# Putting TensorE's instructions into the order of the program text, in a two-block transformer kernel

## The chip, the cores and the metric

The kernel runs on one core of a Trainium2 chip. Its time is the device time of one execution in microseconds; the runs before the change have a median of 1624.3 us. A core has a matrix engine (TensorE, PE in the rows), three engines for elementwise work (VectorE or DVE, ScalarE or ACT, GpSimd or POOL), and SyncE (SP), which here issues the transfers. Each engine works through a list of its own, in the order of that list, and waits at semaphores for the others. The kernel uses PSUM, into which TensorE writes, as eight banks of 128 x 512 fp32; ScalarE and VectorE read the banks out.

## The reference, cut to what matters

Two transformer blocks, one behind the other, on x of 512 tokens by 1024, in fp32:

```
# block 1
h = rms_norm(x, norm1); cols = split(h @ w_in)
y = concat[ short_conv(...), sparse_attention(q, compressed, selected, window keys, gates),
            latent_attention(c_q, c_kv, k_rope), stick_breaking(q, k, v) ]     # 256 columns each
x = x + group_rms_norm(y) @ w_out
x = x + square(relu(rms_norm(x) @ ffn_w1)) @ ffn_w2                            # 4096 hidden
# block 2
o  = gla(q, k_f, f_f, v) + reversed gla(...)        # 4 heads, chunks of 64
o  = rms_norm(o) * silu(g);  y_rec = o @ w_br_rec
qa, ka = partial_rotary(q_a), partial_rotary(k_a)   # 8 query heads, 2 key heads of 64
y_att = window_gqa_sink(qa, ka, va, sink) @ w_br_att
x = x + (sigmoid(gate_r) * y_rec + sigmoid(gate_a) * y_att) @ w_out
x = x + softmax(q @ k.T / 16) @ v @ w_o             # 4 heads over 256 memory tokens
x = x + conv_ffn(rms_norm(x))                       # 2816 hidden
```

In the stick-breaking heads, log(1 - sigmoid) of the logits is summed over the keys to the right of each key. In the sparse attention, blocks of 32 keys and values are compressed by a two-layer network before a first attention looks at them.

## The kernel before, in words

**Precision.** An fp32 product is made of three matmuls on rounded parts, hi x hi, lo x hi and hi x lo, which add up in one PSUM bank (`mm3`, L183 to L185). A part `hi` is a rounded copy by ScalarE (L191, L194, weights L258), a part `lo` the difference, by VectorE (L192, L195, weights L259). Weights come by SyncE's DMAs into three buffers `wraw` and are split there into two pairs `whi`, `wlo` (`wunit`).

**Layout.** A token-major result (tokens on partitions) is turned by TensorE's transposes, four of 128 x 128 into one bank, before it can be used in the next product. `trans_hl` (L854) then splits it with one ScalarE and one VectorE instruction. `trans_pair` (L866) makes operands for two heads from one bank; for each of the two parts ScalarE writes one half of the partitions and VectorE the other half (`split_pair`):

```
for i, s in enumerate("hl"):
    nc.scalar.activation(x[own], b[own], AF.Copy, scale=scale[own])            # L880
    nc.vector.scalar_tensor_tensor(x[oth], b[own], scale[own], x[own], ...)    # L881
```

**Banks.** Four banks with the tag `mm` take the projections. The other four are shared out by phase: two `L` for logits, one `pT` for transposes and one `o` for products with the values in both blocks' mixers. A tile with the same tag that is asked for again waits until the one before it in that bank has been read.

**Order.** The program text is a trace: Python functions issue instructions, and a scheduler then sets each engine's order, by a priority (the place in the trace) and by times that it models. The text interleaves by hand. Long projections are generators (`nproj_g`, `tproj_g`), which `fill`, `weave` and `pipeline` run some steps of between the steps of a head (`attend`: logits, softmax, transposes at L833, values at L844). In `mixers1`, the generator `side` runs beside the stick-breaking heads (first product L913 and L914, sums over keys L934, values L946): it projects queries and values, then two operands of the compression, which go from the bank through VectorE (L636, L637), two DMAs that shift partitions, VectorE (L1175), ScalarE and VectorE into `cB`, and then the compression's matmuls (L1184, L1186) and the projection of keys and values in turns. At its end `nsa_norms` normalises queries and keys (ScalarE, VectorE; the queries at L1015), and `nsa_prep` turns them with `trans_pair`. The generator `side2` runs beside the sparse attention with the convolution and the latent attention's projections. At the end of `mixers1`, `group_out` normalises the last group of columns (`yN`; squares at L785, scaled at L789) and turns it (L798) into H4 and H5, operands of the output projection; that of the group before becomes H6 and H7.

In `mixers2` the linear attention's heads (`gla_head`) are followed by `window`: VectorE rotates part of queries and keys (L1649 to L1652), four `trans_pair` turn the queries (`wq0` to `wq3`), two `trans_hl` the doubled keys (`wkd` to `wk0`, `wk1`), and then logits (L889, L890) and the rest of a head alternate with projections, of `rT` (the recurrent branch), merged with a gate in `M`. Its output `oN` is turned by four `trans_hl` ahead of the product with `w_br_att`.

## Time and profile before

| | us |
|---|---|
| median of 3 runs | 1624.3 (1623.17 to 1624.51) |
| profiled execution | 1626.29 |
| its span | 1624.6 |
| TensorE busy | 1591.5 (98%), 8049 matmuls and transposes |
| VectorE, ScalarE, GpSimd busy | 921.0 (57%), 667.0 (41%), 174.9 (11%) |
| mean DMA rate | 91 GB/s |

The stages by time of the span: first projection and stick-breaking to about 115 us, sparse and latent attention to about 282, first output projection and feed-forward layer to 690, linear attention to 912, window attention and output projection to about 1056, memory attention, and from about 1230 on the second feed-forward layer.

In the timelines below, a row gives start, length, engine, line, operation, output and inputs; in square brackets stands how long the engine had been idle before it and what ended that. Lengths of TensorE's rows overlap, since matmuls are pipelined: the step from one start to the next is what a matmul costs (0.23 us for 512 columns).

### The profile page before, as it was taken

Reading aid. Unit: us, or ns where it says so; the run is one execution under the profiler, and the core shown is the slowest. Engines: PE = TensorE matmul, PEld = TensorE weight load, DVE = VectorE, ACT = ScalarE, POOL = GpSimd, SP = SyncE. Lnnn points to the kernel's source line nnn. Section 1 sums busy time; section 2 is a strip of 40 time slices with the busy share of each in tenths; the row PEclk is TensorE's granted clock in tenths of the full one; section 3 lists DMA queues with packets and bytes.
Section 4 is the critical chain, followed back from the end, with each engine's and each line's share of the span. In section 5 each row is a group of like instructions: output and inputs, shape, how many; then the busy total and the mean of one; then the engine's idle time right before and its main releaser. Section 6 shows DMA issues by size and latency. Waiting matters only on the chain.

```text
span 1624.6 us, 20813 instructions
## 1 busy us (share of the span) xinstructions
PE 1591.5 (98%) x8049; PEld 1341.8 (83%) x8049; DVE 921.0 (57%) x1503; ACT 667.0 (41%) x1172; POOL 174.9 (11%) x185
## 2 busy tenths in 40 slices
PE   8999999999999999999999999999999999999998
PEld 6798888788888888878888788888988888888886
DVE  6666885644223434475766565664667556526662
ACT  5675554544123423334333354353544233222332
POOL 0121110200000001121110000330002111001110
PEclk9999999999999999999999999999999999999999
DMA  7242131232322223221222211323332333232331
GB/s 225 67 126 85 33 117 40 66 102 92 101 94 98 97 94 100 88 89 55 73 72 78 65 40 59 115 96 118 126 98 84 99 98 97 94 101 91 101 120 52
DMA packets 108118, 148.15 MB, mean 91 GB/s; under 512 B 7887, under 2 KB 58868, under 8 KB 108020
## 3 DMA queue, kind: packets, MB, share of 16 engines
q1 hardware_dynamic: 107876, 146.72, 28.3%
q8 instruction: 63, 1.03, 0.3%
q14 instruction: 35, 0.29, 0.1%
q10 hardware_dynamic: 144, 0.11, 0.0%
HBM read 142.31 MB, written 4.20 MB: 90 GB/s over the span
## 4 chain that ended last, share of the span: by engine, by line
PE 90%; DVE 4%; ACT 2%; issue 1%; POOL 1%; DMA 1%; SPq 0%; POOLq 0%; DVEq 0%; ACTq 0%
PE mm L183 25%; PE mm L185 25%; PE mm L184 25%; PE o L844 2%; PE lv L1570 2%; PE pT L833 1%; PE o L1613 1%; DVE wlo L259 1%; ACT whi L258 1%; PE L L889 1%; DMA wraw<-w_in_dram 1%; DMA wraw<-w_down_dram 1%; PE o L183 0%; PE o L185 0%; PE L L890 0%
## 5 line engine op out<-in xcount | busy, mean ns | idle before, releaser
L259 DVE TENSOR_TENSOR wlo<-wraw,whi 128x1024 fp32r<-128x1024 f32 (+4 forms) x268 | 319.5, 1194 | 439.2 <-ACT whi L258 434.5
L258 ACT ACTIVATE whi<-wraw 128x1024 fp32r<-128x1024 f32 (+4 forms) x268 | 270.4, 1010 | 536.9 <-PE mm L184 470.2
L417 POOL TENSOR_TENSOR nacc<-nacc,nsq 128x512 f32<-128x512 f32 x24 | 37.3, 1553 | 508.7 <-ACT nsq L415 507.6
L1866 POOL TENSOR_TENSOR fz<-fz,fu 128x512 f32<-128x512 f32 x22 | 37.4, 1698 | 269.6 <-ACT fz L1865 269.6
L461 DVE TENSOR_TENSOR x<-mm,x 128x512 f32<-128x512 f32 x72 | 48.9, 687 | 19.1 <-PE mm L185 18.8
L183 PE MATMUL mm<-H4h,whi 128*128 128x512 f32 x147 | 59.3, 404 | 0.0
L183 PE MATMUL mm<-H0h,whi 128*128 128x512 f32 x139 | 55.8, 402 | 2.9 <-ACT whi L258 2.9
L183 PE MATMUL mm<-H6h,whi 128*128 128x512 f32 x147 | 58.1, 399 | 0.4 <-ACT H6h L194 0.4
L183 PE MATMUL mm<-H7h,whi 128*128 128x512 f32 x147 | 58.3, 397 | 0.0
L185 PE MATMUL mm<-H4h,wlo 128*128 128x512 f32 x147 | 57.6, 392 | 0.7 <-DVE wlo L259 0.7
L183 PE MATMUL mm<-H5h,whi 128*128 128x512 f32 x147 | 58.1, 395 | 0.0
L185 PE MATMUL mm<-H6h,wlo 128*128 128x512 f32 x147 | 57.7, 393 | 0.0
L185 PE MATMUL mm<-H5h,wlo 128*128 128x512 f32 x147 | 57.7, 393 | 0.0
L184 PE MATMUL mm<-H6l,whi 128*128 128x512 f32 x147 | 57.7, 393 | 0.0
L184 PE MATMUL mm<-H5l,whi 128*128 128x512 f32 x147 | 57.4, 391 | 0.0
L184 PE MATMUL mm<-H4l,whi 128*128 128x512 f32 x147 | 57.4, 391 | 0.0
L185 PE MATMUL mm<-H7h,wlo 128*128 128x512 f32 x147 | 57.4, 390 | 0.0
L184 PE MATMUL mm<-H7l,whi 128*128 128x512 f32 x147 | 57.3, 390 | 0.0
L185 PE MATMUL mm<-H2h,wlo 128*128 128x512 f32 x139 | 54.5, 392 | 1.1 <-DVE wlo L259 1.1
L183 PE MATMUL mm<-H3h,whi 128*128 128x512 f32 x139 | 55.4, 399 | 0.0
L183 PE MATMUL mm<-H2h,whi 128*128 128x512 f32 x139 | 55.2, 397 | 0.0
L183 PE MATMUL mm<-H1h,whi 128*128 128x512 f32 x139 | 54.9, 395 | 0.0
(1264 smaller groups left out, 4340.1 us busy)
## 6 DMA issues: line engine op xcount, KB each, us to landing
wraw<-ffn_w_dram SPq DMA_DIRECT2D x64, 512.0 KB, 3.6
wraw<-w_up_dram SPq DMA_DIRECT2D x88, 256.0 KB, 2.8
wraw<-w_in_dram SPq DMA_DIRECT2D x36, 512.0 KB, 3.4
wraw<-w_down_dram SPq DMA_DIRECT2D x22, 512.0 KB, 3.6
wraw<-w_mem_kv_dram SPq DMA_DIRECT2D x16, 512.0 KB, 3.7
wraw<-w_in_dram SPq DMA_DIRECT2D x52, 128.0 KB, 2.3
wraw<-w_in_dram SPq DMA_DIRECT2D x20, 256.0 KB, 2.8
wraw<-cmp_w_dram SPq DMA_DIRECT2D x8, 512.0 KB, 4.0
```

What stands on the lines that cost most here:

```text
L183: mm(out, a.hi, b.hi, start=start, stop=False, skip_group_check=skip)
L184: mm(out, a.hi, b.lo, start=False, stop=False, skip_group_check=skip)
L185: mm(out, a.lo, b.hi, start=False, stop=stop, skip_group_check=skip)
L258: nc.scalar.activation(hi, raw, AF.Copy)
L259: nc.vector.tensor_sub(lo, raw, hi.bitcast(F32))
L417: eng.tensor_add(nm.acc, nm.acc, sq[:, :nm.N])
L461: self.nc.vector.tensor_add(self.x[k], b, self.x[k])
L833: nc.tensor.transpose(b[:, t * P:(t + 1) * P], st["p"][:, t * P:(t + 1) * P], self.ident)
L844: nc.tensor.matmul(o(), st["pT"][:, t * P:(t + 1) * P], v(t), start=(t == 0), stop=(t == nt - 1))
L889: self.nc.tensor.matmul(out, q[h][:, qs], k.hi[:, ks], start=True, stop=False)
L1570: nc.tensor.matmul(b[:, t * P:(t + 1) * P], ym[:, t * P:(t + 1) * P], mix(X, c, t * P, P), start=True, stop=True)
L1866: nc.gpsimd.tensor_mul(z, z, us[c])
```

## The change

The body of the first mixers behind the first projection, and the four stages that follow, are put into a context of the framework in which the scheduler keeps TensorE's instructions in the order in which the text issues them. The other engines' orders are still found by the scheduler, against the new order of TensorE. Everything else in the diff is indentation; lines behind L536 move by four or five.

```diff
-        self.ffn1()
+        with tc.manual_schedule(engines={mybir.EngineType.PE}):
+            self.ffn1()
...
-        self.mixers2()
+        with tc.manual_schedule(engines={mybir.EngineType.PE}):
+            self.mixers2()
...
-        self.memory()
+        with tc.manual_schedule(engines={mybir.EngineType.PE}):
+            self.memory()
...
-        self.ffn2()
+        with tc.manual_schedule(engines={mybir.EngineType.PE}):
+            self.ffn2()
...
             self.tproj(nm.H, w, [(1772, 512)], ev_sqk)
             self.setup_rest()
-            qN = self.T(mp, [P, NT, 256], F32, "qN")
-            svN = self.T(mp, [P, NT, 256], F32, "svN")
...
+            with tc.manual_schedule(engines={mybir.EngineType.PE}):
+                qN = self.T(mp, [P, NT, 256], F32, "qN")
+                svN = self.T(mp, [P, NT, 256], F32, "svN")
...
```

TensorE's list differs in two stretches, which are the mixers' second part (from about 74 us to the output projection at about 292) and the window attention with what follows (from 912 to about 1010), and in two short places of the memory attention. Three of the places follow, as TensorE's list has them.

TensorE at the start of the window attention, before the change, in part: the transposes of the queries `qkv` into `pT` stand one by one between projection matmuls of `rT0` and `rT1`.

```order
L183 MATMUL mm_7858<-rT0h_6626,whi_7862 128x512
L184 MATMUL mm_7858<-rT0l_6627,whi_7862 128x512
L185 MATMUL mm_7858<-rT0h_6626,wlo_7863 128x512
L183 MATMUL mm_7858<-rT1h_7061,whi_7862 128x512
L866 MATMUL pT_7774<-cmat_78,qkv_5936 128x128
L184 MATMUL mm_7858<-rT1l_7062,whi_7862 128x512
L185 MATMUL mm_7858<-rT1h_7061,wlo_7863 128x512
L866 MATMUL pT_7774<-cmat_78,qkv_5936 128x128
```

The same place after it, from the last transposes of the linear attention (`tr`) to the first projection matmul of `rT0`:

```order
L1639 MATMUL tr_7723<-cmat_78,go_7684 128x128 x4
L871 MATMUL pT_7782<-cmat_78,qkv_5944 128x128 x4
L871 MATMUL pT_7793<-cmat_78,qkv_5944 128x128 x4
L871 MATMUL pT_7804<-cmat_78,qkv_5944 128x128 x4
L871 MATMUL pT_7815<-cmat_78,qkv_5944 128x128 x4
L859 MATMUL pT_7829<-cmat_78,wkd_7826 128x128 x4
L859 MATMUL pT_7841<-cmat_78,wkd_7838 128x128 x4
L894 MATMUL L_7851<-wk0h_7834,wq0h_7787 128x256
L895 MATMUL L_7851<-wk0l_7835,wq0h_7787 128x256
L894 MATMUL L_7859<-wk0h_7834,wq0l_7790 128x256
L895 MATMUL L_7859<-wk0l_7835,wq0l_7790 128x256
L183 MATMUL mm_7865<-rT0h_6634,whi_7870 128x512
```

All 24 transposes of queries and keys moved ahead of the projection matmuls that had stood before and between them.

TensorE at the first step of the compression, before: behind the matmul that ends the projection of the compression's operands stand the sums over keys (L934) of a stick-breaking head.

```order
L185 MATMUL mm_649<-H7h_197,wlo_730 128x512
L934 MATMUL L_674<-sbLh_691,cmatr_81 128x512
L934 MATMUL L_674<-sbLl_692,cmatr_81 128x512
L934 MATMUL L_674<-sbLh_702,cmatr_81 128x384
L934 MATMUL L_675<-sbLh_702,cmatr_81 128x384
```

The same place after:

```order
L185 MATMUL mm_651<-H7h_197,wlo_732 128x512
L1189 MATMUL mm_765<-whi_743,cB_770 64x256
L1191 MATMUL mm_765<-wlo_744,cB_770 32x256
L1189 MATMUL mm_765<-whi_743,cB_770 64x256
L1191 MATMUL mm_765<-wlo_744,cB_770 32x256
L1189 MATMUL mm_765<-whi_743,cB_770 64x256
L1191 MATMUL mm_765<-wlo_744,cB_770 32x256
L1189 MATMUL mm_765<-whi_743,cB_770 64x256
L1191 MATMUL mm_765<-wlo_744,cB_770 32x256
L939 MATMUL L_676<-sbLh_693,cmatr_81 128x512
```

The first eight matmuls of the compression, which read `cB`, moved ahead of the sums over keys and of the next head's logits.

TensorE at the preparation of the sparse attention, before: the transposes of the normalised queries `qN` among projection matmuls that are already at the weights' second unit (`whi_1326`).

```order
L183 MATMUL mm_1322<-whi_1326,H3h_157 128x364
L184 MATMUL mm_1322<-wlo_1327,H3h_157 128x364
L866 MATMUL pT_1334<-cmat_78,qN_427 128x128
L185 MATMUL mm_1322<-whi_1326,H3l_158 128x364
L866 MATMUL pT_1334<-cmat_78,qN_427 128x128
L184 MATMUL mm_1323<-wlo_1327,H2h_147 128x364
```

The same place after:

```order
L1034 MATMUL pT_1275<-sbe_1270,rel_1272 4x384
L1205 MATMUL L_1281<-cmat_78,ev_1222 128x32 x4
L183 MATMUL mm_1323<-whi_1177,H0h_127 128x364
L184 MATMUL mm_1323<-wlo_1178,H0h_127 128x364
L185 MATMUL mm_1323<-whi_1177,H0l_128 128x364
L871 MATMUL pT_1336<-cmat_78,qN_429 128x128 x4
L183 MATMUL mm_1323<-whi_1177,H1h_137 128x364
L184 MATMUL mm_1323<-wlo_1178,H1h_137 128x364
L185 MATMUL mm_1323<-whi_1177,H1l_138 128x364
L871 MATMUL pT_1350<-cmat_78,qN_429 128x128 x4
```

The transposes moved ahead of nearly the whole first unit and part of the second; three matmuls stand ahead of them and three between the two batches.

## Rows read from the trace of the kernel before

**Rows 1.** The page's first part: busy time, share of the span, instructions.
```profile
PE 1591.5 (98%) x8049; PEld 1341.8 (83%) x8049; DVE 921.0 (57%) x1503; ACT 667.0 (41%) x1172; POOL 174.9 (11%) x185
```

**Rows 2.** The page's chain that ended last, by engine.
```profile
PE 90%; DVE 4%; ACT 2%; issue 1%; POOL 1%; DMA 1%; SPq 0%; POOLq 0%; DVEq 0%; ACTq 0%
```

**Rows 3.** Stretches: length, busy time of each engine, clock, DMA share, GB/s.
```profile
40.60:324.90 284.30, 272.55 (x1618) 233.63 (x1617) 193.70 (x466) 171.34 (x396) 52.02 (x85) 0.98 0.25 76
...
893.50:1015.00 121.50, 120.53 (x709) 102.38 (x708) 71.78 (x166) 58.40 (x130) 4.32 (x8) 1.00 0.17 54
```

**Rows 4.** Short stretches of TensorE alone: length, busy, clock, DMA share, GB/s.
```profile
178.00:181.40 3.40, 3.40 (x10) 0.51 0.03 7
283.60:287.10 3.50, 3.50 (x9) 0.52 0.00 0
...
74.05:81.68 7.63, 5.95 (x38) 1.00 0.50 138
```

**Rows 5.** Timeline of TensorE at the start of the window attention.
```profile
912.66 0.59 PE L1634 MATMUL tr<-cmat,go 128*128 128x128 f32 x2 [0.53 <-DVE go L1632]
913.01 0.48 PE L183 MATMUL mm<-rT0h,whi 128*128 128x512 f32 x1
...
929.53 0.63 PE L866 MATMUL pT<-cmat,qkv 128*128 128x128 f32 x4
...
933.31 0.63 PE L866 MATMUL pT<-cmat,qkv 128*128 128x128 f32 x4
```

**Rows 6.** Timelines of VectorE and ScalarE there.
```profile
918.49 0.32 DVE L1652 TENSOR_TENSOR qkv<-qkv,wu 128x160 f32<-128x160 f32 x1
...
930.20 0.69 ACT L880 ACTIVATE wq2h<-pT,w 64x512 fp32r<-64x512 f32 x1 [2.14 <-PE pT L866]
...
930.92 0.74 DVE L881 SCALAR_TENSOR_TENSOR wq2h<-pT,w,wq2h 64x512 fp32r<-64x512 f32 x1 [1.53 <-ACT wq2h L880]
...
931.69 0.68 ACT L880 ACTIVATE wq2l<-pT,w 64x512 fp32r<-64x512 f32 x1 [0.81 <-DVE wq2h L881]
...
932.41 0.76 DVE L881 SCALAR_TENSOR_TENSOR wq2l<-pT,w,wq2l 64x512 fp32r<-64x512 f32 x1 [0.75 <-ACT wq2l L880]
```

**Rows 7.** Timeline of TensorE ahead of the product with `w_br_att`.
```profile
1001.49 0.60 PE L854 MATMUL pT<-cmat,oN 128*128 128x128 f32 x4
...
1003.31 0.40 PE L183 MATMUL mm<-H1h,whi 128*128 128x512 f32 x1
1003.54 0.62 PE L854 MATMUL pT<-cmat,oN 128*128 128x128 f32 x4
```

**Rows 8.** Timeline of TensorE in the stick-breaking heads and the compression.
```profile
69.06 2.34 PE L946 MATMUL o<-svN,sba 128*128 128x64 f32 x20
...
74.05 0.39 PE L934 MATMUL L<-sbLh,cmatr 128*128 128x512 f32 x1
...
77.06 0.38 PE L934 MATMUL L<-sbLl,cmatr 128*128 128x256 f32 x1 [0.49 <-DVE sbLl L192]
...
81.68 0.31 PE L1184 MATMUL mm<-whi,cB 128*64 128x256 f32 x1
```

**Rows 9.** Timelines of TensorE and VectorE at the sparse attention's preparation.
```profile
116.53 0.28 PE L185 MATMUL mm<-whi,H7l 128*128 128x256 f32 x1
...
123.54 0.27 PE L866 MATMUL pT<-cmat,qN 128*128 128x128 f32 x1
...
122.71 1.49 DVE L1015 TENSOR_TENSOR qN<-qN,nrr 128x256 f32<-128x256 f32 x4
```

**Rows 10.** Timelines of TensorE and VectorE at the first mixers' end.
```profile
282.85 0.33 PE L798 MATMUL pT<-cmat,yq 128*128 128x128 f32 x1 [0.37 <-ACT yT L805]
283.60 1.97 PE L183 MATMUL mm<-H6h,whi 128*128 128x512 f32 x4 [0.42 <-ACT H6h L194]
...
291.60 0.48 PE L183 MATMUL mm<-H4h,whi 128*128 128x512 f32 x1
...
287.53 1.15 DVE L789 TENSOR_SCALAR yN<-yN,grs 128x256 f32<-128x256 f32 x4 [1.13 <-POOL grs L226]
```

## The prediction

> **What bounds the kernel now.** I read the page's first part, then its chain, then the table of stretches, and last the timeline at the places where TensorE's work moves. The first part says that TensorE is the bound: busy for 1591.5 of 1624.6 us, with VectorE at 57% and ScalarE at 41% [rows 1], and 90% of the chain that ended last is TensorE [rows 2]. So there is little to win and much to lose: whatever TensorE has to wait for comes straight on top of the time. The stretches tell how little. Between 40.6 and 324.9 us TensorE is idle for 284.30 - 272.55 = 11.8 us, and between 893.5 and 1015 us for 121.50 - 120.53 = 1.0 us [rows 3]. These two stretches are, apart from two short pieces in the memory attention, the only ones where the change gives TensorE another order; in the feed-forward layers and in nearly all of the linear attention the instructions stand as before.

> [...]

> **The change, place by place.** No instruction is added or taken away that counts; TensorE alone is put into the order in which the program was written down. Everything between the other engines stays nearly as it was, so I take durations from the rows and ask at each place what TensorE now has to do while it waits. What it did there before isn't lost: it comes later, so the loss is the work that no longer covers the wait.

> *Start of the window attention, +20 us (13 to 23).* Now six batches of four transposes stand one behind another, with not one projection matmul between them. They all write the one bank `pT`, so each waits until the batch ahead of it has been read out. The rows show one such round without a foreign engine's delay: transposes at 929.53, ScalarE 930.20, VectorE 930.92, ScalarE 931.69 (0.81 us of it waiting for VectorE), VectorE 932.41, next transposes at 933.31 [rows 5, 6]. That is 3.78 us a round. The first batch can't end before the last rotary step of VectorE at 918.49 + 0.32 = 918.81 [rows 6]; VectorE's own order up to there doesn't change. So: batch one at 918.9, ScalarE behind it at 919.2, then 3.11 us of reading out (930.20 to 933.31), so batch two at 922.3, three at 926.1, four at 929.9, the first batch of keys at 933.7. A batch of keys is read out in 1001.49 to 1003.54 = 2.05 us [rows 7], so the second stands at 935.7, the first logits at about 936.2, four of them, and the first projection matmul at about 936.6. Before, it ran at 913.01 [rows 5]. Of these 23.6 us, 24 transposes (0.11 us each) and four logits are work that was done later before, 3.1 us. That leaves 20.5, less half a microsecond of waiting that was there already (0.53 at 912.66). The low end has the rotary steps end 4 us earlier (as far as VectorE's other work could leave their way) and three rounds at 3.1 us, the bare reading out; the high end adds a slow clock during the transposes.

> *Stick-breaking heads and compression, +10 us (4 to 14).* At 74.05 us TensorE went on with the sums over keys of the first head (L934) [rows 8]. Now eight compression matmuls stand ahead of them, and these ran at 81.68, when their operand had passed VectorE, a DMA, VectorE, ScalarE and VectorE again [rows 8]. None of that chain gets shorter. TensorE waits through 7.63 us of which it was busy 5.95 before [rows 4]; by issue intervals (0.23 us for 512 columns, as 1003.31 to 1003.54 [rows 7]) that work is 4.4 us, so +4.4. For the next heads the chain from the end of the logits (69.06) to the last operand of L934 (77.06) is 8.0 us [rows 8]. The cover now standing in it is the value product (2.3 us [rows 8]), sixteen compression matmuls and six of 256 columns (2.6 us) in one head, and in the other the value product and eighteen matmuls (2.1), plus 0.8 us of L934 that needs only the first two operands. That leaves 2.3 and 2.8 us. Weight units of eight short matmuls may add another microsecond, since splitting one takes longer than using it. 4.4 + 2.3 + 2.8 + 0.5 = 10. The low end is the first wait alone; the high end has the heads at their bare 8 us less the value product.

> *Preparation of the sparse attention, +9 us (5 to 12).* The last value matmul of the projection starts at 116.53; the first transposes of the normalised queries stand at 123.54, as soon as VectorE has the first of four tiles (from 122.71) [rows 9]. In between, TensorE did projection matmuls that have 364 columns. Now only some 1.5 us of work stand ahead of the transposes: 7.0 - 1.5, less what VectorE and ScalarE may be earlier, is 4 to 5 us. The second batch waits for a round of 3.78 us with 0.4 us of transposes and 0.5 of matmuls in it: 2.8. The next two wait 1.5 and 0.7 by the same count. Low: the first wait alone; high: every round bare.

> *End of the first mixers, +5 us (3 to 7).* Eight transposes of the last group's output now stand ahead of 24 matmuls (H6, H7) that ran while the group was being normalised. TensorE gets there at 282.85; VectorE scales the four tiles at 287.53 to 288.68 [rows 10]. So it waits to 288.7, then a round of 2.05 us less 0.4 before the second four, and the 24 matmuls (5.4 us) end at about 296.7 where the next ones began at 291.6: 5.1.

> *Transposes in front of the attention's output projection, +5 us (3 to 6).* Four batches back to back where seven matmuls stood between two: 3 x (2.05 - 0.44) = 4.8 [rows 7].

> *Latent-attention projections and memory attention, +4 us (0 to 8).* Five transposes or products one behind another around 172 to 178 us and two places where an output bank is asked for again at once; at most a round of 2.05 us each, mostly covered by what stands between. I take 2 and 2.

> *The clock, +4 us (0 to 9).* The new waits will drop the clock two or three times more than before, at 1.7 us each; none at the low end, five times at the high one.

> *What is won back, -5 us (-12 to 0).* Waits and slow stretches of the old order in the places that change: 11.8 + 1.0 us of idle time and two stretches at 1.7 are 16.2 at most. Most of it sits at chains that stay as long as they are (the 0.49 us at 77.06 [rows 8]), so I take a third.

> **Sum.** 20 + 10 + 9 + 5 + 5 + 4 + 4 - 5 = 52. The profiled execution took 1626.29 us, so 1678.3; it is 2.0 above the median of the runs (1624.3), so 1676 for a median.

> **The rivals.**
> *The other engines catch up (1645 us).* VectorE, ScalarE and SyncE are ordered by the scheduler, and it knows TensorE's order: it can put the work that TensorE waits for ahead of weight splits. For it: VectorE is idle 43% of the time, so there is room. Against it: its order in the window's first 20 us is the old one, and the rounds are chains through one bank that no order shortens. The low ends with something won back, 13 + 4 + 5 + 3 + 3 + 0 + 0 - 7 = 21, give 1645.
> *The stalls feed on each other (1702 us).* High ends, with little won back: 23 + 14 + 12 + 7 + 6 + 8 + 9 - 1 = 78, so 1702. For it: two stretches at half clock stand in the old order already [rows 4], the second right behind waits of 0.37 and 0.42 us [rows 10]. Against it: in 74.05 to 81.68 TensorE was idle for 1.7 us and its clock stayed at 1.00 [rows 4]. [...]
> *Faster (1612 us).* The written order was interleaved by hand: projections are handed out between the steps of the heads, so it could keep TensorE busier than the scheduler's modelled times do. Its price is at most the 16.2 us above; three quarters of it is 12. It decides only if the six batches of the window find their data ready, and they can't before 918.81. So it needs the window's term under some 6 us and all others near nothing.
> *The change does nothing (1624 us).* It would have to leave TensorE's order alone; it does in 60% of the span, but not at the places above.

> **How the numbers follow.** Forecast case (1655 to 1695): 0.65. Others catch up: 0.16. Stalls feed on each other: 0.13. Faster: 0.03. Nothing: 0.03. 1676 is the first. The range goes from 1644 to 1698 and leaves out the faster cases, the lower part of the second and the upper of the third, about 0.19. A change of 0.2% (3 us) is about what can be told from none; slower by more has 0.94, within it 0.03, faster by more 0.03.

> **What would show it right or wrong.** In the new profile: TensorE idle for 18 us or more in the 25 us behind the last linear-attention transposes, its rounds 3 to 4 us apart and ended by ScalarE or VectorE; a wait of some 7 us at 74 us for `cB`; one of 4 us before the query transposes near 118 us and one of 5 to 6 near 283 us (both later by what was lost before); the feed-forward stretches free of idle time as before; PEclk below 1.0 behind the waits. I am wrong if the window's transposes have projection matmuls between them in time, if the wait before the compression is under 3 us, or if idle time in the unchanged stretches differs.

## The result: 1719.2 us, 5.8% slower

The changed kernel takes 1719.16 us (median of 4 runs, 1718.26 to 1719.29) against 1624.4 us for the kernel before on the same chip: a ratio of 1.0584, 95% interval [1.0566, 1.0602]. That is 43 us above the forecast of 1676 and 21 us above the end of its range. The sign was right, the size was not.

The first part of the page of the changed kernel gives busy time, share of the span and count for each engine, and its fourth part the chain that ended last; they answer to [rows 1] and [rows 2].

```profile
PE 1617.3 (94%) x8049; PEld 1360.2 (79%) x8049; DVE 926.0 (54%) x1503; ACT 669.4 (39%) x1172; POOL 168.0 (10%) x185
...
PE 82%; DVE 8%; issue 4%; ACT 3%; DMA 2%; POOL 1%; SPq 1%; POOLq 0%; DVEq 0%; ACTq 0%
```

These two numbers already split the loss. The span grew from 1624.6 to 1717.5 us, by 92.9. For the same 8049 instructions TensorE was busy 1617.3 - 1591.5 = 25.8 us longer: 23.5 of that goes with a lower granted clock, as the next table shows. Its idle time grew from 33.1 to 100.2 us, by 67.1: those are the waits. My sum had 4 and 48 for the two.

Next, the table of stretches. The first two rows are the two stretches of [rows 3] as they stand now (from and to the same instructions); columns are length, busy time of PE, PEld, DVE, ACT and POOL, granted clock, DMA share and GB/s.

```profile
40.80:373.50 332.70, 284.59 (x1614) 241.98 (x1615) 195.74 (x463) 170.38 (x394) 47.16 (x85) 0.93 0.21 65
943.60:1094.50 150.90, 127.64 (x708) 108.09 (x708) 72.15 (x166) 59.90 (x130) 3.57 (x8) 0.90 0.14 43
```

Idle time of TensorE went from 11.8 to 48.1 us in the first, and from 1.0 to 23.3 us in the second. The following rows are the same view of the stretches of the changed kernel in which the granted clock stood at its lower level: 0.50 in slices of one microsecond, 0.50 to 0.57 as the means of the stretches, which hold the edges. The last two or three microseconds of the span, where TensorE has no work left, are low in both kernels (0.50) and are set apart; four stretches of 3.4 us, full of work, are left out, the sum is over all eleven.

```profile
77.80:84.60 6.80, 4.28 (x18) 3.96 (x19) 3.44 (x7) 1.38 (x3) 0.00 (x0) 0.53 0.47 149
...
135.50:145.70 10.20, 5.85 (x23) 4.36 (x24) 6.25 (x15) 4.44 (x10) 4.39 (x13) 0.50 0.34 92
207.40:217.60 10.20, 9.84 (x34) 7.97 (x35) 5.27 (x18) 2.23 (x8) 0.00 (x0) 0.51 0.06 21
...
326.60:336.80 10.20, 5.70 (x17) 4.48 (x18) 3.23 (x8) 2.42 (x7) 1.02 (x1) 0.50 0.01 2
...
964.60:991.90 27.30, 10.09 (x34) 6.88 (x35) 12.55 (x30) 9.29 (x15) 1.50 (x5) 0.51 0.07 20
...
1169.50:1176.30 6.80, 4.67 (x11) 3.74 (x12) 2.67 (x4) 0.39 (x1) 1.04 (x1) 0.51 0.00 0
1282.80:1289.60 6.80, 6.63 (x28) 6.36 (x29) 1.66 (x4) 1.14 (x4) 0.00 (x0) 0.53 0.22 75
sum 91.90, PE 60.66 PEld 49.58 DVE 43.27 ACT 25.48 POOL 8.97; mean PE 5.51 PEld 4.51 DVE 3.93 ACT 2.32 POOL 0.82
```

There are eleven such stretches of 91.9 us with 60.7 us of TensorE's work in them. Taking half of that work as the price, they cost about 30 us: products of 512 columns start 0.43 us apart at the lower level (1175.18 to 1175.61 us) and 0.23 apart at 1.00 (1165.40 to 1165.63). The kernel before had four of 3.4 us at 0.50 to 0.52, full of work (two are in [rows 4]), which cost 6.8. The difference, 23.5, is close to the 25.8 of the page.

Last, the list of what TensorE waited for (total, times, longest).

```profile
PE mm L1189 <- DVE cB L192: 7.2, 1, 7.2
PE pt L439 <- DVE nsq L437: 5.2, 1, 5.2
PE pT L871 <- DVE qN L1020: 5.1, 1, 5.1
PE pT L803 <- DVE yN L794: 4.9, 1, 4.9
...
PE pT L859 <- DVE wq3l L886: 3.3, 1, 3.3
PE pT L871 <- DVE wq0l L886: 3.2, 1, 3.2
...
PE o L183 <- DVE H3l L192: 2.8, 1, 2.8
PE pT L838 <- ACT sbe L842: 2.5, 4, 1.5
PE mm L183 <- ACT mla_p L194: 2.2, 1, 2.2
```

The first, third and fourth are the waits that I had put at `cB`, at the query transposes and at the last group, close to the lengths I gave them (7, 4 to 5, 5 to 6 us). The second, in the memory attention, I had not seen.

To see where the delay is picked up, I took the start of each TensorE instruction after minus before; the clock's part of a place is half of the busy time in its slow stretches, less the same before.

| place | delay gained | clock in it | the rest | forecast for the rest |
|---|---|---|---|---|
| stick-breaking and compression | 15.0 | 3.8 | 11.2 | 10 |
| preparation of the sparse attention | 13.0 | 2.9 | 10.1 | 9 |
| sparse and latent attention | 14.6 | 3.3 | 11.3 | 2 |
| end of the first mixers | 7.1 | 1.2 | 5.9 | 5 |
| start of the window attention | 23.0 | 5.0 | 18.0 | 20 |
| transposes ahead of the output projection | 6.4 | 1.7 | 4.7 | 5 |
| memory attention | 13.1 | 5.7 | 7.4 | 2 |
| everything else | 0.7 | 0 | 0.7 | -5 (won back) |

The last row is made of 1.2 us by which this execution runs ahead at 20 us, 1.5 us lost in the linear attention and some 0.4 us lost behind the memory attention.

### The profile page after: what moved, and what is told of

It is laid out like the page before. It is cut to its first block, busy times and chain, and to the rows that moved or that the text cites. A ratio compares the mean times of both kernels' runs of the same rounds, so it can differ in the third digit from the quotient of the medians.

```text
span 1717.5 us, 20826 instructions
## 1 busy us (share of the span) xinstructions
PE 1617.3 (94%) x8049; PEld 1360.2 (79%) x8049; DVE 926.0 (54%) x1503; ACT 669.4 (39%) x1172; POOL 168.0 (10%) x185
## 4 chain that ended last, share of the span: by engine, by line
PE 82%; DVE 8%; issue 4%; ACT 3%; DMA 2%; POOL 1%; SPq 1%; POOLq 0%; DVEq 0%; ACTq 0%
PE mm L183 23%; PE mm L185 23%; PE mm L184 23%; PE o L849 2%; DVE wlo L259 1%; PE lv L1575 1%; PE pT L838 1%; ACT whi L258 1%; PE o L1618 1%; PE L L939 1%; PE L L894 1%; DMA wraw<-w_down_dram 1%; PE L L895 0%; PE o L183 0%; PE o L185 0%
## 5 line engine op out<-in xcount | busy, mean ns | idle before, releaser
L258 ACT ACTIVATE whi<-wraw 128x1024 fp32r<-128x1024 f32 (+4 forms) x268 | 270.3, 1010 | 551.8 <-PE mm L184 480.5
L1871 POOL TENSOR_TENSOR fz<-fz,fu 128x512 f32<-128x512 f32 x22 | 37.3, 1695 | 269.5 <-ACT fz L1870 269.5
L461 DVE TENSOR_TENSOR x<-mm,x 128x512 f32<-128x512 f32 x72 | 49.1, 688 | 23.5 <-PE mm L185 23.0
```

What stands on the lines that cost most here:

```text
L258: nc.scalar.activation(hi, raw, AF.Copy)
L461: self.nc.vector.tensor_add(self.x[k], b, self.x[k])
L1871: nc.gpsimd.tensor_mul(z, z, us[c])
```

## The experiments

### One part of the change at a time

In four kernels only one stage keeps TensorE's written order; all others lose it by edits like this one:

```
-        with tc.manual_schedule(engines={mybir.EngineType.PE}):
-            self.mixers2()
+        self.mixers2()
```

First mixers: 

> TensorE in the order of the text only in the first mixers behind the first projection; all other stages as before. If each place costs what the two traces show there (49.8 us of delay between 74 and 300 us of the old span, less 1.2 won at the start), the time is 1624 + 48 = 1672. If the losses of one stage depend on the others (for instance because the later stages recover some of it), it is under 1660 or over 1685.

Second mixers: 

> The order of the text only in linear attention and window attention. Places that stand for themselves: 1.5 + 23.0 + 6.4 = 31 us, so 1655. If the window's cost hung on delays brought along from the first mixers: 1640 or less.

Memory attention: 

> The order of the text only in the memory attention with the projection in front of it. Places that stand for themselves: 6.8 + 5.8 + 0.6 = 13 us, so 1637. My prediction's term for this stage was 2 us, so 1626; if the 13 us came from buffers or transfers displaced by earlier stages, it is there.

Both feed-forward layers: 

> The order of the text only in the two feed-forward stages. Both theories: no change, 1624 (within 2); a cost of the context itself, by semaphores or otherwise, would show here as over 1627.

Measured, against 1625.44 us for the kernel before: 1675.33 (ratio 1.0303 [1.0273, 1.0333]), 1656.19 (1.0186 [1.0156, 1.0215]), 1635.19 (1.0063 [1.0040, 1.0086]) and 1626.57 (1.0007 [0.9996, 1.0018]). The four differences, 49.9, 30.8, 9.8 and 1.1, make 91.6, and the whole change costs 94.8: the parts add up to within some 3 us, each with its own clock loss (mean granted clock 0.984, 0.986, 0.994 and 0.996). The two mixers and the feed-forward layers came as expected (1672, 1655, 1624). The memory attention costs 3 us less than the 13 expected, but far more than the forecast's 2.

### The first mixers in quarters

The kernel before, with the written order in one quarter of the first mixers, by these lines ahead of it and behind it. This was done when the 14.6 us of the sparse and latent attention still had no cause.

```
+            cm = tc.manual_schedule(engines={mybir.EngineType.PE})
+            cm.__enter__()
...
+            cm.__exit__(None, None, None)
```

Stick-breaking heads: 

> The kernel before, with TensorE in written order only in the stick-breaking heads and what runs beside them (40 to 114 us), the scheduler's order elsewhere. If each stretch pays for its own order: 12 us slower, 1637. If the work behind it takes up part of the delay: under 8 us.

Preparation of the sparse attention: 

> Written order only from the end of the heads through the preparation of the sparse attention (114 to about 150 us). If each stretch pays for its own order: 15 us slower, 1640. If the measured 15 us were in part handed down from the heads: under 10.

Sparse and latent attention: 

> Written order only in the sparse and the latent attention (about 150 to 275 us). If the 14 us of this stretch are waits of its own order: 1636 to 1640. If they are handed down from the stretches ahead, whose filler steps it lacks: under 5 us slower, 1625 to 1630.

End: 

> Written order only at the end of the first mixers (from the last group's normalisation). If each stretch pays for its own order: 8 us slower, 1633. The forecast's term for this place was 5.

Measured, against 1624.96: 1641.96 (1.0107 [1.0078, 1.0136]), 1634.73 (1.0066 [1.0043, 1.0089]), 1637.32 (1.0079 [1.0049, 1.0108]) and 1630.77 (1.0037 [1.0021, 1.0053]). So 17.0, 9.8, 12.4 and 5.8 us, together 45.0 of the 49.9, where 12, 15, 12 to 16 and 8 were expected. In the first, 2.1 of the 17.0 us are there by 48 us, most of them from a stretch at the lower clock (0.50 from 44 to 47 us), where the changed kernel's execution stands at 1.00. The second, 9.8, is by its time a case for losses handed down from the heads (under 10). Its trace says otherwise: TensorE waits 5.03 and 2.24 us for the two batches of query transposes, against 5.13 and 2.23 in the changed kernel; only the 1.8 us of waits for `kvN` ahead of them are missing. The third quarter costs 12 us by itself, so its waits are not handed down. Its rows say the same. TensorE's timeline in the changed kernel (start, length, line, and in brackets how long it had been idle and for whom):

```profile
196.07 0.70 PE L1119 MATMUL pT<-vbd,npc 128*128 128x256 f32 x2 [0.52 <-DVE sbe L844]
...
201.33 0.66 PE L803 MATMUL pT<-cmat,yN 128*128 128x128 f32 x4 [0.52 <-ACT sbe L842]
...
207.12 0.79 PE L183 MATMUL mm<-whi,mla_p 128*128 128x512 f32 x1 [2.24 <-ACT mla_p L194]
...
231.70 0.70 PE L1119 MATMUL pT<-vbd,npc 128*128 128x256 f32 x2 [1.34 <-DVE sbe L844]
...
254.57 0.66 PE L838 MATMUL pT<-cmat,sba 128*128 128x128 f32 x4 [1.49 <-ACT sbe L842]
```

And in the kernel with the written order in the third quarter alone:

```profile
169.78 0.70 PE L1117 MATMUL pT<-vbd,npc 128*128 128x256 f32 x2 [0.52 <-DVE sbe L842]
...
175.04 0.66 PE L801 MATMUL pT<-cmat,yN 128*128 128x128 f32 x4 [0.52 <-ACT sbe L840]
...
180.83 0.50 PE L183 MATMUL mm<-whi,mla_p 128*128 128x512 f32 x1 [2.24 <-ACT mla_p L194]
...
202.85 0.70 PE L1117 MATMUL pT<-vbd,npc 128*128 128x256 f32 x2 [1.34 <-DVE sbe L842]
...
225.72 0.66 PE L836 MATMUL pT<-cmat,sba 128*128 128x128 f32 x4 [1.49 <-ACT sbe L840]
```

The same waits, to a hundredth of a microsecond, 26.3 us earlier, and 28.9 us earlier from 202.85 on. The step between the two is the clock: behind the same wait for `mla_p` it stays low for 10.2 us in the changed kernel (0.51, the row from 207.40) and for 3.4 us here (0.50 from 183 to 185 us). The waits belong to that stretch's order: fifteen places where a transpose or a product stands right behind what feeds it. The same stretch in the kernel before and in this one (length and busy times; the stretch ends at the same instruction):

```profile
165.00:245.00 80.00, 75.94 (x464) 65.28 (x462) 63.65 (x181) 47.42 (x116) 13.72 (x16) 0.96 0.24 76
```

```profile
165.00:257.30 92.30, 78.90 (x477) 66.89 (x476) 67.76 (x185) 48.25 (x117) 13.13 (x16) 0.96 0.21 66
```

TensorE idles 13.4 us in place of 4.1 at the same mean clock of 0.96.

### The window's rounds

Both kernels are otherwise as the changed one. In the first, the projections are queued ahead of the window attention, and `WF` says how many of their steps are written behind each batch of transposes:

```
+WF = (8, 5, 5, 5, 5, 3, 3)
...
+            self.fill(WF[c])
```

> The changed kernel, with 34 steps of the projections written between the transposes of the window attention (8 ahead of the first batch, 5 between batches of queries, 5 and 3 at the keys, 3 behind) in place of none. Theory one, uncovered waits: what stood between the transposes in the old order is back, so the window's 23 us fall to 2 or less, 1698. Theory two, the chain of rotary steps and reading out is the bound wherever the projections stand: 1715 or more.

In the second, the four batches of queries go to different banks:

```
-            qT += self.trans_pair(wp, [qkv[:, t, c * P:(c + 1) * P] for t in range(NT)], eighth, f"wq{c}")
+            qT += self.trans_pair(wp, [qkv[:, t, c * P:(c + 1) * P] for t in range(NT)], eighth, f"wq{c}",
+                                  ps=("pT", "L", "o", "L")[c])
```

> The changed kernel, with the four batches of query transposes written to the banks pT, L, o, L in place of pT alone; nothing else. If the single bank sets the round: transposes no longer wait, ScalarE and VectorE work on different banks at once, 1.5 us a batch in place of 4.2, so some 8 us less with the clock, 1711. If ScalarE and VectorE are the bound with their 2.9 us a batch whatever the banks: 1716 to 1719.

Measured: 1700.09 us (1.0457 [1.0426, 1.0487]) and 1706.46 us (1.0496 [1.0465, 1.0526]), so 19.1 and 12.7 us less than the changed kernel's 1719.16. The first came as its first case had it, the second lies below both of its cases. Timeline of TensorE in the changed kernel:

```profile
968.91 0.47 PE L871 MATMUL pT<-cmat,qkv 128*128 128x128 f32 x1 [1.14 <-DVE qkv L1657]
972.62 1.09 PE L871 MATMUL pT<-cmat,qkv 128*128 128x128 f32 x4 [3.23 <-DVE wq0l L886]
976.85 1.09 PE L871 MATMUL pT<-cmat,qkv 128*128 128x128 f32 x4 [3.15 <-DVE wq1l L886]
981.09 1.09 PE L871 MATMUL pT<-cmat,qkv 128*128 128x128 f32 x4 [3.15 <-DVE wq2l L886]
985.43 1.09 PE L859 MATMUL pT<-cmat,wkd 128*128 128x128 f32 x4 [3.25 <-DVE wq3l L886]
988.02 1.09 PE L859 MATMUL pT<-cmat,wkd 128*128 128x128 f32 x4 [1.50 <-DVE wk0l L192]
```

Each round waits some 3.2 us for VectorE's last instruction on the bank, as the forecast said; but a batch lasts 1.09 us and not 0.63 [rows 5], and a round 4.23 and not 3.78. The kernel with steps between them, in its row of stretches:

```profile
965.00:992.00 27.00, 24.69 (x119) 19.72 (x119) 19.96 (x37) 10.96 (x16) 1.75 (x6) 1.00 0.28 79
```

TensorE works through 24.7 of 27 us, at a granted clock of 1.00. So rounds through one bank with nothing beside them are the cause of this place: cover gave back 19.1 us, more banks 12.7, two thirds of that. By the starts of TensorE's instructions 16.8 and 11.6 us of the two gains come in the window and the transposes behind it. Another 2.7 us in each come at the changed kernel's row from 1282.80, where neither kernel was edited. TensorE waits 2.76 us for `H3l` there in all three executions, but in these two the clock stays up. The kernel with steps between, with that wait inside, at 1.00:

```profile
1262.00:1272.00 10.00, 7.24 (x53) 6.66 (x52) 5.30 (x10) 4.07 (x10) 0.00 (x0) 1.00 0.32 105
```

So the same wait of 2.76 us has a slow stretch behind it in one execution and none in the other two, and 2.7 us of difference between the kernels come from that alone.

### The clock by itself

114 products of 512 columns that nobody reads are written into the bank `o` where TensorE waits (sparse preparation, end of the first mixers, window, memory broadcast). They add work and shorten no chain.

```
+        b = self.ps("o") if n else None
+        for _ in range(n):
+            self.nc.tensor.matmul(b, x[:, 0:P], x, start=True, stop=True)
```

> The changed kernel, with 114 matmuls of 512 columns added whose result nobody reads: in the waits of the sparse attention's preparation (16, 6, 3), of the first mixers' end (12, 5), of the window attention (8, 10, 10, 10, 10, 4) and ahead of the memory's token broadcast (18). They are 26 us of work put into 45 us of waits; no wait is shortened. Theory clock: the slow clock behind these waits costs half of the 27 us in which TensorE works at it there, so the time falls by 10 to 13 us, to 1706 to 1709, with more work. Theory waits alone: the waits make up the loss, the added work lies inside them or sticks out, 1719 to 1725.

Measured: 1713.80 us (1.0541 [1.0510, 1.0571]), 5.4 less than the changed kernel and between its two cases. Its timeline at the window's batches, then its stretch:

```profile
972.48 0.63 PE L873 MATMUL pT<-cmat,qkv 128*128 128x128 f32 x4 [0.94 <-DVE wq0l L894]
972.86 2.56 PE L880 MATMUL o<-rT0h 128*128 128x512 f32 x10
976.25 0.63 PE L873 MATMUL pT<-cmat,qkv 128*128 128x128 f32 x4 [0.83 <-DVE wq1l L894]
976.64 2.56 PE L880 MATMUL o<-rT0h 128*128 128x512 f32 x10
980.03 0.63 PE L873 MATMUL pT<-cmat,qkv 128*128 128x128 f32 x4 [0.84 <-DVE wq2l L894]
```

```profile
968.00:986.00 18.00, 13.92 (x67) 10.22 (x65) 7.32 (x11) 6.06 (x9) 1.49 (x4) 0.99 0.11 30
```

With useless work in the gaps the clock stays up (0.99) and the round is 3.77 us, the figure of [rows 5]. A round at the lower level (0.51) is 0.46 us longer. So the clock of these rounds goes with what TensorE does in them: at 0.51 it waits, and in between it only transposes. The added products end both at once, and which of the two counts no run separates. Over the whole kernel the mean clock rose from 0.973 to 0.987 and the cost of the slow stretches (busy half) fell from 30 to 19 us, yet only 5.4 us came back where the clock's theory had more: the delay gained fell by 0.4 us in the sparse preparation, 2.4 at the end of the mixers, 2.6 in the window and its transposes and 3.2 in the memory attention, and this execution reached the first mixers 2.5 us later. One reason is that such a place waits for chains of VectorE and ScalarE, which hardly got shorter: in the sparse preparation, from the start of the query transposes to the end of VectorE's `sqk0l`, 4.56 us pass in the changed kernel and 4.44 in this one. The other is the added work itself. TensorE's idle time fell from 100.2 to 77.2 us, by 23.0 us for 26.2 us of added products, while its busy time rose by only 16.5 (1617.3 to 1633.8), so 9.7 us of the clock's cost came back there and 3.2 were lost again beside it. That the clock costs something is shown; that all of the longer busy time could be had back is not, and at the places tried it could not.

### The wait in the memory attention

In one kernel the broadcast is written nine steps into the next projection. In the other its VectorE tile gets a buffer of its own:

```
-        dg = self.T(self.sp, [P, NT, P], F32, "nsq", 2)[:, :nt]
+        dg = self.T(self.sp, [P, NT, P], F32, "nsq", 2)[:, :nt] if pool is None else self.T(pool, [P, nt, P], F32, "dg", 1)
...
-                mn.R = self.token_bcast(mn.rs, 256, "pt")
+                mn.R = self.token_bcast(mn.rs, 256, "pt", kp)
```

Broadcast later: 

> The changed kernel, with the memory's token broadcast issued 9 steps into the first key projection, as late as the old order had it, in place of 12 matmuls ahead of that projection. If the wait at 1171 us is uncovered chain: 5.2 us of wait and the slow clock behind it go, 1712 to 1713. If the chain ends late whatever is issued in the meantime: 1719.

Own buffer: 

> The changed kernel, with the broadcast tile of the memory attention's norm in a buffer of its own instead of one shared with the square sums. If the 5.16 us wait of TensorE at the broadcast comes from VectorE waiting for GpSimd to release that buffer, the wait falls under 1.5 us, the 6.8 us stretch at half clock behind it goes, and the time is 1711 to 1714 us. If the chain before the broadcast is late by itself, the wait stays over 3 us and the time is 1717 or more.

Measured: 1717.17 us (1.0562 [1.0531, 1.0592]) and 1711.49 us (1.0536 [1.0482, 1.0589], runs 6 us apart). The first is a miss: 2.50 us of the wait are left at L439, 1.48 us for weights came in ahead of it, and behind the place TensorE is 0.2 us later against the changed kernel than ahead of it. The 2.0 us that its time shows came elsewhere, most of them at the `H3l` wait of 1283 us, whose slow stretch it lacks. The second is a hit, though not by its time alone, since its interval reaches over the changed kernel's 1.0584: in the trace the wait and the slow stretch are gone, and the place gives back 7.3 us. The timelines of GpSimd and VectorE in the changed kernel show why:

```profile
1161.14 0.70 POOL L226 TENSOR_TENSOR rs<-rst,mhalf 128x2 f32<-128x2 f32 x1 [4.42 <-DVE rst L209]
1167.89 2.65 POOL L417 TENSOR_TENSOR nacc<-nacc,nsq 128x512 f32<-128x512 f32 x2 [6.04 <-ACT nsq L415]
```

```profile
1169.24 1.39 DVE L437 TENSOR_SCALAR nsq<-cmat,rs 128x128 f32<-128x128 f32 x1 [1.16 <-POOL nacc L417]
```

The number `rs` that VectorE needs is there at 1161.84, but its output tile shares two buffers with the square sums of the next norm and gets one when GpSimd has used it, seven microseconds later. GpSimd had itself been waiting 6.04 us for ScalarE's squares in that buffer. In the kernel with its own buffer VectorE starts with `rs`, and TensorE waits for nothing (no bracket):

```profile
1159.84 0.48 DVE L437 TENSOR_SCALAR dg<-cmat,rs 128x128 f32<-128x128 f32 x2 [0.82 <-POOL rs L226]
```

```profile
1164.28 0.59 PE L439 MATMUL pt<-dg,ones 128*128 128x256 f32 x2
```

The kernel before has a wait of 1.56 us at this place. So I also gave the tile its own buffer there.

> The kernel before, with the broadcast tile of the memory attention's norm in a buffer of its own. If the 1.56 us wait of TensorE there comes from the shared buffer as it does in the changed kernel, 1.5 us go: 1623 us, ratio 0.999. If the scheduler covers it with other work anyway, no change: 1624.5.

Measured: 1624.8 us, ratio 0.9995 [0.9986, 1.0004]. The wait is gone from its trace, but one of 1.00 us for weights (`wlo`) stands 7 us further on, and the time did not change by what can be told.

### Mending the written order

Three kernels on top of the changed one. In the first, two filler steps of the first stick-breaking head move behind its sums over keys of the next one:

```
-                    self.fill(10)
+                    self.fill(12 if h == 1 else 10)
...
-                    self.fill(6)
+                    self.fill(4 if h == 0 else 6)
```

> The changed kernel, with two filler steps of the first stick-breaking head's score stage moved to the second head's, and so the steps that read cB come later in TensorE's order. If the 7.24 us wait for cB is a matter of a place in the order only, it shrinks by about 4 us with 2 us of clock beside it: 1713 us. If the later waits of that stage (attention's DVE chain) set it, they grow by as much: 1719.

1716.62 us (1.0567 [1.0537, 1.0598]): between the two. The wait for `cB` fell from 7.24 to 2.40 us, with new waits of 0.68 and 0.91 us at L939 ahead of it. By the starts of TensorE's instructions the place gave 5.2 us, and nothing was lost behind it. What hides the gain was lost ahead of the edit: this execution is 2.5 us later than the changed kernel's by 72 us, 1.6 of them through a stretch at the lower clock (0.50) that the other does not have:

```profile
44.20:47.60 3.40, 3.40 (x10) 2.64 (x9) 3.33 (x5) 2.30 (x3) 0.13 (x1) 0.50 0.17 39
```

The kernel with the written order in the first mixers alone, with no edit of the steps, shows the same stretch.

In the second, four steps stand between the latent attention's transposes and their use, in place of one:

```
-                    yield
+                    for _ in range(4):
+                        yield
```

> The changed kernel, with the latent attention's transposes and the projection that reads them four steps apart in the written order instead of one. If the 2.24 us wait for mla_p is what drops the clock at 207 to 218, both go: 1712 us. If only the wait goes, 1717. If the wait moves to what was put between, 1719.

1719.0 us (1.0582 [1.0551, 1.0613]): no change, the last of the three cases. The wait for `mla_p` is not among its waits between 190 and 290 us; in their place stand these, of which the first was not among the changed kernel's, the second was 1.3 and the third 0.5:

```profile
PE mm L426 <- POOL nacc L993: 3.1, 1, 3.1
PE mm L439 <- DVE nsq L437: 2.6, 1, 2.6
PE pT L839 <- DVE sbe L845: 2.3, 1, 2.3
```

The third kernel mends all places found: filler between the window's batches, in the sparse preparation, at the end of the mixers and between the output transposes, with three edits from above (own buffer, moved steps, four steps).

> TensorE still in written order everywhere, with the written order mended at seven places: window, sparse preparation, end of the first mixers, output transposes, memory broadcast, stick-breaking score stage and latent attention. If the cost of the change is waits at places where the written order puts a reader right behind its writer, and the clock that those waits cost, the mended places give back 19 us (window, measured), 15 (sparse preparation), 8 (end of mixers), 4 (output transposes), 6 (broadcast) and 5 more: near 1669 us, 1655 to 1685. If the loss is carried by VectorE and ScalarE being late as a whole, the waits come back further on: over 1690.

1683.98 us (1.0367 [1.0332, 1.0401]): 35.2 us less than the changed kernel, 15 short of what the places promised and at the upper end of the expected range. Its first mixers (the stretch of [rows 3]) and the place of its longest wait:

```profile
42.00:368.40 326.40, 284.83 (x1614) 242.64 (x1615) 196.21 (x464) 171.24 (x394) 48.48 (x85) 0.94 0.22 67
```

```profile
199.99 1.22 PE L1127 MATMUL pT<-vbd,npc 128*128 128x256 f32 x2 [4.95 <-DVE sbe L852]
```

TensorE still idles 41.6 us there (48.1 in the changed kernel, 11.8 before). The steps handed to the sparse preparation were taken from the sparse attention, which now waits 4.95 us at a place where it waited 0.5 before (and 0.52 with the latent attention's edit alone): its delay grew by 4.0 us while the preparation gained 3.2, since there a wait of 4.36 us stands ahead of a product of the compression in place of the one of 5.13 for `qN`. Filler steps are a fixed stock, and spending them earlier leaves the later waits bare. What the best written order would give stays open; none that I tried reaches the scheduler's.

## Why the prediction was wrong

**Right: the sign, and the five chains that I followed in the trace.** Stick-breaking 10 (11.2 measured, without the clock's part), sparse preparation 9 (10.1), end of the mixers 5 (5.9), window 20 (18.0), output transposes 5 (4.7). The rounds through one bank and the waits for `cB`, `qN` and `yN` are in the trace as described, and the first of the window's rounds ran back to VectorE's rotary steps. TensorE idled 18.5 us in the 25 us behind the last linear-attention transposes (18 or more was the sign), but a round took 4.23 us, not 3 to 4. In the stick-breaking term luck had a part: the operands of the sums over keys in the later heads, put at 2.3 and 2.8 us, were waited for some 1.2 us in all, and split weights, put at 0.5, for 4.7. What a reader can keep: follow one operand from engine to engine, then subtract the work still standing beside it.

**Wrong: the step "The clock, +4 us".** The page shows 25.8 us more busy time, and the slow stretches make 23.6 of them (the third column of the table). I had priced each new drop at 1.7 us, half of the two short stretches of [rows 4] at 0.51 and 0.52, and put two or three more of them down; no run shows that term. Eleven stretches came in place of four, and they are longer: one of 27.3 us lies over the whole row of window batches. I had even used the round of 3.78 us, with the lower level only as the high end; at 0.51 the round took 4.23. The case that I held against the rival, 1.7 us of idle time in 7.6 at a clock of 1.00 [rows 4], could not carry that weight: at 178 us the clock fell to 0.51 behind less idle time than that. The row of the 8 us ahead shows 0.9 us of it, nearly all in one wait:

```profile
170.00:178.00 8.00, 7.07 (x52) 5.90 (x52) 5.84 (x13) 5.28 (x14) 2.98 (x2) 1.00 0.00 1
```

TensorE's last 6 us there were transposes and products of 256 columns or fewer; at 74 us it had products of 512 columns among them. Idle time alone did not tell these two places apart, and I had counted nothing else. In the window the clock did not come back up between the batches, it stayed at 0.51 over all six of them. But the clock is not a separate bill: in the kernel with useless products the cost of the slow stretches fell by 11 us and the time by 5.4. Nor does a wait always bring it, as the window kernels show behind the 2.76 us for `H3l`.

**Wrong: the step "Latent-attention projections and memory attention, +4 us".** 11.3 and 7.4 us, without the clock's part. I had looked for changed order at five transposes around 172 to 178 us, and taken the rest of the sparse and latent attention as interleaved by hand and so as covered. The quarter run alone costs 12.4 us, in fifteen waits of 0.3 to 2.2 us; the kernel before has four there, of 0.4 to 1.4 us, because the scheduler fills the others with something else. Of the memory attention's 7.4, 3.6 are the wait for the broadcast (5.2 us against 1.56 before), which is a shared buffer's and not a chain's, and 2.8 the wait for `H3l`, whose cause stays open.

**Wrong: the step "What is won back, -5 us".** Nothing: no place of the table has less delay than it began with, the last row is 0.7 and not below 0, and the feed-forward layers' 1.1 us is not to be told from none. The old idle time sat at chains that kept their length, as I had argued for most of it.

Together, by the table: 23.6 - 4 = 19.6 us for the clock, 14.7 for the attentions, 5.7 for what was not won back and 0.9 at the five chains, 40.9. The remaining 2 of the 43 were taken off in the forecast because the profiled execution stood above the median, and did not show again. The rival "stalls feed on each other" (1702) was nearer, but for part of its reasons: its bounds for the clock (9) and the attentions (8) were far too low, and those for the five chains too high. I had set these bounds by the rows of before, and rows of before cannot show a wait that the scheduler had already filled.

## What to carry to other kernels

A scheduler's order is worth what its fillings are worth: before one engine is put into written order, count every place in the text where a reader stands right behind its writer, the short ones too. Price each run of waits twice, as idle time (67.1 us more here) and as the lower clock in the work between (23.5 us more here), but do not add up the two without asking what waits behind. Read a gain of 2 or 3 us at its place in the trace and not from the time alone, since a slow stretch elsewhere can come or stay away (2.7 us at `H3l`). Filler is a stock: moving it to the longest wait pays only if the place it came from did not need it.
